# RMS-norm squares kept in fp32 and added in pairs on the vector engine, and buffer slots claimed by the first operation, in an eight-core hybrid decoder step

## The chip, the cores and the metric

The kernel runs on all 8 cores of one Trainium2 chip. Every core runs the same program on its own eighth of the batch: one prompt of 2048 tokens and 16 single-token samples. The metric is device time in microseconds (us) of the slowest core, in one launch. A run can fall into a slow state, in which one die (cores 0 to 3, or 4 to 7) is granted a lower TensorE clock; only fast runs are compared here.

The engines are named as the profile names them: PE is TensorE (matmuls; PEld its weight loads), DVE is VectorE, ACT is ScalarE, POOL is GpSimd, SP issues DMAs.

## The reference, cut to what matters

Four layers, then a final norm. D is 1024, the feed-forward width 2816.

```python
def _rmsnorm(x, g):
    xf = x.astype(jnp.float32)
    y = xf * lax.rsqrt(jnp.mean(xf * xf, axis=-1, keepdims=True) + RMS_EPS)
    return (y * g.astype(jnp.float32)).astype(x.dtype)

# one layer
    h = _rmsnorm(x, norm1_g)                      # "first norm" (n1)
    z = h @ w_in
    zb, zc, zv, zu, ga, gs = jnp.split(z, cuts, axis=-1)
    conv_out, new_buf = _conv_causal(zc * zv, conv_buf, conv_w, conv_b)
    ya = zb * conv_out
    ys, hr, hi = _s5(zu, ...)                     # diagonal state space (SSM)
    gy = jax.nn.gelu(ys, approximate=False)
    ys = gy * jax.nn.sigmoid(gy @ w_glu + b_glu)
    m = jax.nn.sigmoid(ga) * (ya @ w_branch[:512]) + jax.nn.sigmoid(gs) * (ys @ w_branch[512:])
    x = x + m @ w_out
    h2 = _rmsnorm(x, norm2_g)                     # "second norm" (n2)
    gate, up = jnp.split(h2 @ w_gate_up, [D_FF], axis=-1)
    x = x + (jax.nn.silu(gate) * up) @ w_down
```

## The kernel before

Each core keeps x in SBUF in fp32 (tile X), transposed: 128 partitions times 8 chunks of the 1024 model channels, tokens along the free axis. It works through the prompt in two halves of about 1024 tokens. The first half also carries the 16 samples and is cut into three blocks of 384, 384 and 272 columns; the second half into two blocks of 512. A norm therefore has to sum over partitions, which it does with matmuls by a matrix of ones:

```python
    def norm(half, blk, l, which, src=None):
        xin = src or (lambda kt: (X[:, kt, blk.c0:blk.c0 + n], xkeys(kt, blk)))
        ps = PP.new()
        n = blk.n
        hq = lambda kt: (R if which == "fg" else H)[:, kt, blk.c0:blk.c0 + n]     # bf16
        qkeys = rkeys if which == "fg" else hkeys
        for kt in range(8):
            act(lambda e, kt=kt: e.activation(out=hq(kt), in_=xin(kt)[0], func=AF.Square),
                xin(kt)[1], qkeys(kt, blk), n)
            S.pe([(lambda e, kt=kt: e.matmul(ps[:, 0:n], lhsT=ONESB[:], rhs=hq(kt), start=(kt == 0), stop=(kt == 7)),
                   qkeys(kt, blk) + [C_("ONESB")], MMN(n))], [(ps,)], FULL)
        rs = SP_.new()
        # rs = exp(-0.5 * ln(sum / D + eps)): two activations of the "ln" table set
        act(... func=AF.Ln ...); act(... func=AF.Exp, scale=-0.5 ...)
        ...
        for kt in range(8):                       # the "scaling": H = X * g * rs, on DVE
            dve(lambda e, ...: e.scalar_tensor_tensor(out=H[:, kt, ...], in0=xi(), scalar=g, in1=rs[:, 0:n], ...), ...)
```

So a block's norm is 8 squares on ACT (rounded to bf16 into H), 8 ones-matmuls on PE, Ln and Exp on ACT, 8 scalings on DVE, which overwrite H with the normalised input of the next projections.

Nothing is in program order. The operations are recorded with the tiles that they read and write, and a list scheduler orders each engine's queue when the kernel is built. A tile from a pool (`TP` has 4 slots of TB, `SP_` 5 and `SQ` 4 of SC, `PP` the 8 PSUM banks) gets its slot when the first operation that names it is placed; until a slot is free, no operation that names the tile can be placed. The gate projections of the convolution branch are evicted to TB tiles:

```python
            for jj in range(4):
                t_ = tj[jj] = TP.new()
                for blk in blks:
                    pg = projh(uga[jj // 2], jj % 2, blk)      # 8 matmuls into a PSUM bank
                    act(lambda e, ...: e.activation(out=t_[:, ...], in_=pg[:, 0:blk.n], func=AF.Sigmoid), [(pg,)], [(t_, blk.i)], blk.n, tset="sig")
```

The matmuls do not name `t_`, so the scheduler may place them while no TB slot is free, and their PSUM banks then wait full.

Each layer also needs tables for the SSM (complex products of powers of the diagonal). `prep(l)` computes them on DVE and GpSimd with `tt` (fp32 tensor-tensor operations), for layer 0 at the start of the kernel, for the later layers under the feed-forward part of the layer before, in the first half only:

```python
                if half == 0 and l + 1 < DEPTH:
                    span = len(S.ops) - ffn0
                    prep(l + 1, ((ffn0, ffn0 + PS1 * span), (ffn0 + PS1 * span, ffn0 + 0.8 * span)))
```

Of the kernel before, what the change touches and what calls it, by code (L numbers as in the profile page):

```python
# [10 lines left out]
ALU = mybir.AluOpType  # L11
# [65 lines left out]
class Prog:  # L77
    ENGS = ("pe", "act", "dve", "pool", "sp")
    LAT = 0.07
    SWITCH = 1.28  # L80
    MODESW = 0.16
    DBW = 300.0e3
# [94 lines left out]
    def schedule(self):  # L177
# [54 lines left out]
        while nleft:  # L232
# [4 lines left out]
            if isinstance(e, tuple):  # L237
                p, s = e
# [91 lines left out]
                    push(tl.end + self.LAT, (p, tl.slot))  # L330
            for s, i in o.succ:
                s.npred -= 1
                r = o.end + (0.0 if e == "pe" and s.eng == "pe" else self.LAT) - s.offs[i]
                if r > s.ready:
                    s.ready = r
                if s.npred == 0:
                    heapq.heappush(fut[s.eng], (s.ready, s.seq, s))
                    push(max(s.ready, t, efree[s.eng]), s.eng)
# [122 lines left out]
def build():  # L461
# [199 lines left out]

    FULL = (128, 128)

    def proj(parts, blk):
        ps = PP.new()
        nmm = len(parts)
        subs = []
        for i, (u, kw, c, src, keys) in enumerate(parts):
            subs.append((lambda e, u=u, kw=kw, c=c, src=src, i=i: e.matmul(  # L669
                ps[:, 0:blk.n], lhsT=u.ap(kw, c), rhs=src(blk), start=(i == 0), stop=(i == nmm - 1)),  # L670
                [u.key] + keys(blk), MMN(blk.n)))
        S.pe(subs, [(ps,)], FULL)
        return ps

# [9 lines left out]
    def rk(t):  # L684
        return lambda blk: rkeys(t, blk)

    def projh(u, mt, blk):
        return proj([(u, k, mt * 128, hsrc(k), hk(k)) for k in range(8)], blk)

    def projr(u, c, slots, blk):  # L690
        return proj([(u, k, c, rsrc(t), rk(t)) for k, t in enumerate(slots)], blk)
# [1 line left out]
    def norm(half, blk, l, which, src=None):  # L693
        xin = src or (lambda kt: (X[:, kt, blk.c0:blk.c0 + n], xkeys(kt, blk)))
        ps = PP.new()
        n = blk.n
        hq = lambda kt: (R if which == "fg" else H)[:, kt, blk.c0:blk.c0 + n]
        qkeys = rkeys if which == "fg" else hkeys
        for kt in range(8):
            act(lambda e, kt=kt: e.activation(out=hq(kt), in_=xin(kt)[0], func=AF.Square),  # L700
                xin(kt)[1], qkeys(kt, blk), n)
            S.pe([(lambda e, kt=kt: e.matmul(ps[:, 0:n], lhsT=ONESB[:], rhs=hq(kt), start=(kt == 0), stop=(kt == 7)),  # L702
                   qkeys(kt, blk) + [C_("ONESB")], MMN(n))], [(ps,)], FULL)
        rs = SP_.new()
        act(lambda e: e.activation(out=rs[:, 0:n], in_=ps[:, 0:n], func=AF.Ln, bias=CST[:, 0:1], scale=1.0 / D),
            [(ps,), C_("CST")], [(rs,)], n, tset="ln")
        act(lambda e: e.activation(out=rs[:, 0:n], in_=rs[:, 0:n], func=AF.Exp, scale=-0.5), [(rs,)], [(rs,)], n, tset="ln")  # L707
        for kt in range(8):
            xi = lambda kt=kt: xin(kt)[0]
            xik = xin(kt)[1]  # L710
            if which == "fg":
                g = PRM[:, PFG + kt:PFG + kt + 1]
                npr = blk.np
                dve(lambda e, xi=xi, g=g: e.scalar_tensor_tensor(
                    out=xi(), in0=xi(), scalar=g, in1=rs[:, 0:n], op0=ALU.mult, op1=ALU.mult),
                    xik + [(rs,), pk], xik, n, dur=STT_(n), prio=len(S.ops) + (FO if half == 0 else 0))
                S.dma("sp", lambda e, kt=kt: e.dma_start(out=yT[half, :, kt, blk.c0:blk.c0 + npr], in_=X[:, kt, blk.c0:blk.c0 + npr]),
                      [k_ for k_ in xik if k_[2] != 8], [], 128 * npr * 4)
        if which == "fg" and 8 in blk.ss:
            S.dma("sp", lambda e: e.dma_start(out=ysT, in_=X[:, :, 1024:1040]), [("X", k, 8) for k in range(8)], [], 65536)  # L720
        if which != "fg":
            for kt in range(8):
                xi = lambda kt=kt: xin(kt)[0]
                xik = xin(kt)[1]
                g = pcol(l, which, kt)
                dve(lambda e, kt=kt, xi=xi, g=g: e.scalar_tensor_tensor(  # L726
                    out=H[:, kt, blk.c0:blk.c0 + n], in0=xi(), scalar=g, in1=rs[:, 0:n], op0=ALU.mult, op1=ALU.mult),
                    xik + [(rs,), pk], hkeys(kt, blk), n, dur=STT_(n))
# [18 lines left out]
    def prep_body(l):  # L747
# [100 lines left out]
        def prep_f(f):  # L848
# [10 lines left out]
            for h in range(2):  # L859
# [2 lines left out]
                bn16 = lambda bn=bn: bn[:, 0:512].bitcast(BF16).rearrange("p (q r c) -> p q r c", q=4, r=2)  # L862
                bno = lambda ri, bn16=bn16: bn16()[:, :, ri, :].rearrange("p q (c s) -> p q c s", c=16)
                o8 = 8 * h
                tt(zz1, lambda: Bv(me, 0), lambda o8=o8: Pv(pw, o8), ALU.mult, bkk, [(z1,)], 512)
                tt(zz2, lambda: Bv(bct, 256), lambda o8=o8: Pv(me, 512 + o8), ALU.mult, bkk, [(z2,)], 512)
                tt(lambda bno=bno: bno(0), zz1, zz2, ALU.subtract, [(z1,), (z2,)], [(bn, 0)], 512)
                tt(zz2, lambda: Bv(bct, 0), lambda o8=o8: Pv(pw, 256 + o8), ALU.mult, bkk, [(z2,)], 512)
# [109 lines left out]
    def layer(half, l, after_blk, before_fd2=None):  # L978
# [173 lines left out]
        def gas(j4):  # L1152
            uga = [next_unit("ga") for _ in range(2)]
            for jj in range(4):
                t_ = tj[jj] = TP.new()
                for blk in blks:
                    pg = projh(uga[jj // 2], jj % 2, blk)
                    act(lambda e, t_=t_, pg=pg, blk=blk: e.activation(out=t_[:, blk.c0:blk.c0 + blk.n], in_=pg[:, 0:blk.n], func=AF.Sigmoid),  # L1158
                        [(pg,)], [(t_, blk.i)], blk.n, tset="sig")
        for f0 in range(2):  # L1160
# [256 lines left out]
```

## Time and profile before

| | before |
|---|---|
| time, median (range) | 3663.6 us (3660.8 to 3669.5), 3 runs |
| PE busy on the slowest core | 3504.0 us, 96% |
| DVE, ACT, POOL busy | 44%, 31%, 17% |
| ones-matmuls of the norms | 360 |
| waits of PE with a named releaser, mean of the cores | 90.4 us |

These are the lines of the page of the kernel before: the summary of busy times by engine (busy us, share of the span, number of instructions), the clock row of the 40 slices (tenths of full speed), the chain that ended last by line, and the groups of the norm: scaling, squares and ones-matmuls (out<-in, shapes, count | busy us, mean ns of one | idle before and its releaser).

```profile
...
PE 3504.0 (96%) x23912; PEld 1979.7 (54%) x23912; DVE 1618.6 (44%) x2889; ACT 1141.7 (31%) x2151; POOL 608.7 (17%) x799
...
PEclk9799999999999999999999999999999999999999
...
PE ps L669 83%; DMA yT<-X 1%; PE ps L702 1%; PE ps L1107 1%; DVE SC L561 1%; DVE H L726 1%; PE ps L1033 1%; PE ps L908 1%; PE ps L1080 0%; DVE X L1246 0%; DMA scv<-CIN 0%; SPq L632 0%; PE ps L895 0%; DMA X<-xsT 0%; DVE R L1225 0%
...
L700 ACT ACTIVATE H<-X 128x384 bf16<-128x384 f32 (+2 forms) x304 | 156.6, 539 | 198.4 <-DVE X L1246 178.7
L726 DVE SCALAR_TENSOR_TENSOR H<-X,PRM,SC 128x384 bf16<-128x384 f32 (+2 forms) x304 | 183.0, 672 | 35.0 <-ACT SC L707 34.8
...
L702 PE MATMUL ps<-H,ONESB 128*128 128x384 bf16 (+2 forms) x320 | 78.1, 348 | 27.5 <-ACT H L700 26.8
...
```

PE is the bound: 83% of the chain is the projection matmuls of L669. DVE and ACT have more than half of the time free, so work can move from PE to DVE if it does not end up in front of a PE instruction. The ones-matmuls of the squares in H took 78.1 us of PE. The clock row shows one slice below 9: slice 2, about 92 to 183 us, layer 0's table preparation.

These are the waits of PE in layer 0 between its two norms (waiting instruction <- releaser: us in total, times, longest us), and the busy time by engine in 50 to 140 us (start:end length, then busy us and instructions of PE, PEld, DVE, ACT and POOL, the granted clock, DMA share, GB/s).

```profile
...
PE ps L895 <- DVE SC L561: 12.5, 9, 3.0
...
PE ps L895 <- ACT R L775: 6.0, 1, 6.0
PE ps L895 <- ACT TAB L775: 5.8, 1, 5.8
...
```

```profile
...
50.00:140.00 90.00, 51.80 (x592) 34.02 (x592) 83.69 (x128) 37.16 (x74) 34.57 (x30) 0.75 0.50 116
...
```

DVE, which makes the tables, was busy for 83.69 of 90 us, PE for 51.80 of them at a clock of 0.75.

This is the timeline of the last block of a second norm in the first half (start us, length us, engine, line, operation, count, idle before <- releaser).

```profile
...
301.28 0.43 ACT L707 ACTIVATE SC<-SC 128x272 f32<-128x272 f32 x1
...
304.50 1.53 POOL L561 TENSOR_TENSOR TB<-TB 128x512 f32<-128x512 f32 x1 [1.01 <-ACT TAB L889]
...
305.49 1.09 DVE L561 TENSOR_TENSOR TAB<-SC 128x512 bf16<-128x512 f32 x1
306.24 1.47 POOL L561 TENSOR_TENSOR TAB<-TB 128x512 bf16<-128x512 f32 x1 [0.20 <-POOL TB L561]
306.50 5.20 DVE L726 SCALAR_TENSOR_TENSOR H<-X,PRM,SC 128x272 bf16<-128x272 f32 x8
307.84 1.08 POOL L561 TENSOR_TENSOR TB<-TB 128x512 f32<-128x512 f32 x1
...
308.25 0.28 PE L669 MATMUL ps<-H,RING 128*128 128x272 bf16 x1 [2.38 <-DVE H L726]
...
309.37 6.94 PE L669 MATMUL ps<-H,RING 128*128 128x272 bf16 x25 [0.84 <-DVE H L726]
...
```

PE stood still for 2.38 and 0.84 us until the scalings had filled H. Their factor rs was ready long before: its Exp (L707) ended at 301.71. The first scaling began 4.8 us later, because DVE still had preparation (L561) and feed-forward work placed ahead of it in its queue.

### The profile page before, as it was taken

What the parts mean: (1) busy time and instruction counts of PE and PEld (TensorE: products, weight loads), DVE (VectorE), ACT (ScalarE), POOL (GpSimd) and SP (SyncE); (2) the same over time, 40 slices, a digit from 0 to 9 for tenths busy, and PEclk for the clock granted to TensorE, in tenths of its full rate; (3) what the DMA queues carried; (4) which work ended last, traced back from release to release, by engine and by line L of the source; (5) the groups of instructions that cost most, each with busy time, mean ns of one, the idle gap of its engine ahead of it and who ended that gap; (6) DMA issues with size and microseconds to landing.
All of it is one profiled execution on the core that took longest, in us unless ns stands there. A gap on an engine that the chain in (4) does not pass through costs nothing.

```text
span 3663.7 us, 67385 instructions; the slowest of 8 cores (3647.5 to 3663.7 us)
## 1 busy us (share of the span) xinstructions
PE 3504.0 (96%) x23912; PEld 1979.7 (54%) x23912; DVE 1618.6 (44%) x2889; ACT 1141.7 (31%) x2151; POOL 608.7 (17%) x799
## 2 busy tenths in 40 slices
PE   6699999999999999999999899999999999999998
PEld 3466666666666666666664344444444444444443
DVE  8745555465454654543244331354224442254313
ACT  4443234332353322533134320243103421042202
POOL 4232210322103221030000200002000110002000
PEclk9799999999999999999999999999999999999999
DMA  7444557435574355854338544574445644474443
GB/s 157 115 82 70 114 139 149 87 66 113 138 155 86 62 113 135 185 110 84 70 71 196 116 77 71 98 169 74 75 77 115 144 70 81 70 146 79 79 72 87
DMA packets 252804, 384.14 MB, mean 105 GB/s; under 512 B 157632, under 2 KB 180800, under 8 KB 246848
## 3 DMA queue, kind: packets, MB, share of 16 engines
q0 software_dynamic: 67968, 243.30, 39.5%
q1 hardware_dynamic: 184512, 136.53, 12.8%
q8 instruction: 202, 3.31, 0.4%
q14 instruction: 122, 1.00, 0.1%
HBM read 567.06 MB, written 56.12 MB: 170 GB/s over the span
## 4 chain that ended last, share of the span: by engine, by line
PE 88%; DVE 4%; issue 3%; DMA 3%; ACT 1%; SPq 1%; DVEq 0%; ACTq 0%; POOL 0%; POOLq 0%
PE ps L669 83%; DMA yT<-X 1%; PE ps L702 1%; PE ps L1107 1%; DVE SC L561 1%; DVE H L726 1%; PE ps L1033 1%; PE ps L908 1%; PE ps L1080 0%; DVE X L1246 0%; DMA scv<-CIN 0%; SPq L632 0%; PE ps L895 0%; DMA X<-xsT 0%; DVE R L1225 0%
## 5 line engine op out<-in xcount | busy, mean ns | idle before, releaser
L669 PE MATMUL ps<-H,RING 128*128 128x512 bf16 (+2 forms) x12160 | 2194.9, 340 | 23.5 <-DVE H L726 9.7
L669 PEld LDWEIGHTS ps<-H,RING 128*128 128x128 bf16 x12160 | 1191.5, 99 | 965.9 <-issue 52.3
L669 PE MATMUL ps<-R,RING 128*128 128x384 bf16 (+2 forms) x6400 | 1162.1, 339 | 19.7 <-DMA R<-dy 11.4
L669 PEld LDWEIGHTS ps<-R,RING 128*128 128x128 bf16 x6400 | 624.2, 98 | 517.8 <-issue 35.4
L656 POOL DMA_DIRECT2D RING<-wpk x472 | 253.0, 537 | 2635.0 <-PE ps L669 2431.7
L1268 DVE TENSOR_TENSOR R<-SC,ps 128x384 bf16<-128x384 f32 (+2 forms) x440 | 255.8, 583 | 786.7 <-PE ps L669 773.6
L1267 ACT ACTIVATE SC<-ps 128x384 f32<-128x384 f32 (+2 forms) x440 | 226.1, 515 | 1208.0 <-PE ps L669 1199.6
L1246 DVE TENSOR_TENSOR X<-X,ps 128x384 f32<-128x384 f32 (+2 forms) x480 | 269.8, 582 | 448.2 <-PE ps L669 445.2
L700 ACT ACTIVATE H<-X 128x384 bf16<-128x384 f32 (+2 forms) x304 | 156.6, 539 | 198.4 <-DVE X L1246 178.7
L726 DVE SCALAR_TENSOR_TENSOR H<-X,PRM,SC 128x384 bf16<-128x384 f32 (+2 forms) x304 | 183.0, 672 | 35.0 <-ACT SC L707 34.8
L1240 POOL TENSOR_TENSOR R<-TB,SC 128x384 bf16<-128x384 f32 (+1 forms) x160 | 168.1, 1063 | 113.1 <-DVE SC L1237 101.4
L1237 DVE TENSOR_TENSOR SC<-SC,ps 128x384 f32<-128x384 f32 (+1 forms) x160 | 92.7, 584 | 163.5 <-PE ps L669 78.6
L1236 ACT ACTIVATE SC<-ps 128x384 f32<-128x384 f32 (+1 forms) x160 | 81.4, 515 | 248.2 <-PE ps L669 219.8
L1213 DVE TENSOR_TENSOR TB<-TB,ps 128x384 f32<-128x384 f32 (+2 forms) x160 | 89.9, 582 | 128.6 <-PE ps L669 124.6
L1172 DVE TENSOR_TENSOR CIN<-ps,SC 128x384 f32<-128x384 f32 (+2 forms) x80 | 47.0, 587 | 200.7 <-ACT SC L1171 192.6
L561 DVE TENSOR_TENSOR SC<-TB 128x512 f32<-128x512 f32 (+1 forms) x160 | 124.1, 785 | 8.1 <-PE ps L908 0.6
L1158 ACT ACTIVATE TB<-ps 128x384 f32<-128x384 f32 (+1 forms) x160 | 78.9, 516 | 85.8 <-PE ps L669 85.4
L702 PE MATMUL ps<-H,ONESB 128*128 128x384 bf16 (+2 forms) x320 | 78.1, 348 | 27.5 <-ACT H L700 26.8
L561 POOL TENSOR_TENSOR TB<-TB 128x512 f32<-128x512 f32 (+1 forms) x72 | 89.3, 1242 | 42.3 <-DVE R L835 20.7
L1225 DVE TENSOR_TENSOR R<-R,SC 128x384 bf16<-128x384 bf16 (+2 forms) x80 | 46.4, 588 | 88.8 <-ACT SC L1223 86.7
L899 ACT ACTIVATE TAB<-ps 128x512 bf16<-128x512 f32 x60 | 35.5, 597 | 133.0 <-PE ps L895 132.8
L1171 ACT ACTIVATE SC<-ps 128x384 f32<-128x384 f32 (+2 forms) x80 | 41.0, 513 | 95.7 <-PE ps L669 95.5
(180 smaller groups left out, 1633.1 us busy)
## 6 DMA issues: line engine op xcount, KB each, us to landing
RING<-wpk POOLq DMA_DIRECT2D x440, 512.0 KB, 7.0
TAB<-stash SPq DMA_DIRECT2D x21, 1792.0 KB, 10.0
stash<-TAB SPq DMA_DIRECT2D x15, 1792.0 KB, 7.6
R<-stash SPq DMA_DIRECT2D x7, 1792.0 KB, 14.8
RING<-wpk POOLq DMA_DIRECT2D x32, 384.0 KB, 6.1
du<-R SPq DMA_DIRECT2D x32, 256.0 KB, 9.2
UU<-du SPq DMA_DIRECT2D x32, 256.0 KB, 7.2
dy<-YY SPq DMA_DIRECT2D x32, 256.0 KB, 6.6
```

The costliest lines, as they stand in the source:

```text
L561: fn = lambda e: e.tensor_tensor(out=out(), in0=a(), in1=b(), op=op)
L656: S.dma("pool", lambda e: e.dma_start(out=t[:, 0:n], in_=wpk[l, ui, :, 0:n]), [("X",) + gate] if gate else (), [(t,)], 128 * n * 4, prio=- ...
L669: subs.append((lambda e, u=u, kw=kw, c=c, src=src, i=i: e.matmul(ps[:, 0:blk.n], lhsT=u.ap(kw, c), rhs=src(blk), start=(i == 0), stop=(i = ...
L700: act(lambda e, kt=kt: e.activation(out=hq(kt), in_=xin(kt)[0], func=AF.Square), xin(kt)[1], qkeys(kt, blk), n)
L702: S.pe([(lambda e, kt=kt: e.matmul(ps[:, 0:n], lhsT=ONESB[:], rhs=hq(kt), start=(kt == 0), stop=(kt == 7)), qkeys(kt, blk) + [C_("ONESB")] ...
L726: dve(lambda e, kt=kt, xi=xi, g=g: e.scalar_tensor_tensor(out=H[:, kt, blk.c0:blk.c0 + n], in0=xi(), scalar=g, in1=rs[:, 0:n], op0=ALU.mul ...
L1213: dve(lambda e, po=po, n=n, t_=t_, blk=blk: e.tensor_tensor(out=t_[:, blk.c0:blk.c0 + n], in0=t_[:, blk.c0:blk.c0 + n], in1=po[:, 0:n], op ...
L1237: dve(lambda e, sg=sg, po=po, n=n: e.tensor_tensor(out=sg[:, 0:n], in0=sg[:, 0:n], in1=po[:, 0:n], op=ALU.mult), [(sg,), (po,)], [(sg,)], n)
L1240: S.op(MENG, lambda e, sg=sg, n=n, t_=t_, blk=blk, j=j: e.tensor_tensor(out=R[:, MT[j], blk.c0:blk.c0 + n], in0=t_[:, blk.c0:blk.c0 + n], ...
L1246: dve(lambda e: e.tensor_tensor(out=X[:, j, blk.c0:blk.c0 + n], in0=X[:, j, blk.c0:blk.c0 + n], in1=ps[:, 0:n], op=ALU.add), [(ps,)] + xke ...
L1267: act(lambda e, sg=sg, pg=pg, n=n: e.activation(out=sg[:, 0:n], in_=pg[:, 0:n], func=AF.Silu), [(pg,)], [(sg,)], n, tset="silu")
L1268: dve(lambda e, sg=sg, pu=pu, n=n, blk=blk, ti=ti: e.tensor_tensor(out=R[:, ti, blk.c0:blk.c0 + n], in0=sg[:, 0:n], in1=pu[:, 0:n], op=ALU ...
```

## The change

The intent is to halve the ones-matmuls: the squares of two chunks are kept in fp32 (in SC tiles), added on DVE, rounded once into bf16, and one ones-matmul takes the sum. Left as they were are the first norm of layer 0 (the start), the norm at the change of halves that reads a staged input, and the final norms. Besides, an operation that fills a PSUM bank for a TB slot now names the TB tile ("own"), so that it is placed only when the slot is there. `LATPE` has the value of `LAT` and changes nothing.

```diff
-    def proj(parts, blk):
+    def proj(parts, blk, own=()):
 ...
-                [u.key] + keys(blk), MMN(blk.n)))
+                [u.key] + keys(blk) + list(own), MMN(blk.n)))
 ...
+        pairs = which != "fg" and src is None and not (half == 0 and l == 0 and which == "n1")
+        QP = SQ if half == 1 else SP_
+        for k2 in range(4 if pairs else 0):
+            ta, tb2 = QP.new(), QP.new()
+            for t, kt in ((ta, 2 * k2), (tb2, 2 * k2 + 1)):
+                act(lambda e, kt=kt, t=t: e.activation(out=t[:, 0:n], in_=xin(kt)[0], func=AF.Square), xin(kt)[1], [(t,)], n)
+            tt(lambda k2=k2: hq(k2), lambda ta=ta: ta[:, 0:n], lambda tb2=tb2: tb2[:, 0:n], ALU.add, [(ta,), (tb2,)], qkeys(k2, blk), n)
+            S.pe([(lambda e, k2=k2: e.matmul(ps[:, 0:n], lhsT=ONESB[:], rhs=hq(k2), start=(k2 == 0), stop=(k2 == 3)),
+                   qkeys(k2, blk) + [C_("ONESB")], MMN(n))], [(ps,)], FULL)
-        for kt in range(8):
+        for kt in range(0 if pairs else 8):
 ...                                              # table preparation
-                tt(zz1, ..., ALU.mult, bkk, [(z1,)], 512)
+                tt(zz1, ..., ALU.mult, bkk + [(tab, "own")], [(z1,)], 512)
 ...                                              # gate projections
-                    pg = projh(uga[jj // 2], jj % 2, blk)
+                    pg = projh(uga[jj // 2], jj % 2, blk, [(t_, "own")])
```

More of the change, by code (lines that the diff above doesn't have):

```diff
@@ L79 @@
     LAT = 0.07
+    LATPE = 0.07
     SWITCH = 1.28
@@ L332, in schedule @@
                 s.npred -= 1
-                r = o.end + (0.0 if e == "pe" and s.eng == "pe" else self.LAT) - s.offs[i]
+                r = o.end + (0.0 if e == "pe" and s.eng == "pe" else self.LATPE if s.eng == "pe" else self.LAT) - s.offs[i]
                 if r > s.ready:
@@ L685, in rk, with projh @@
         return lambda blk: rkeys(t, blk)
-    def projh(u, mt, blk):
-        return proj([(u, k, mt * 128, hsrc(k), hk(k)) for k in range(8)], blk)
+    def projh(u, mt, blk, own=()):
+        return proj([(u, k, mt * 128, hsrc(k), hk(k)) for k in range(8)], blk, own)
     def projr(u, c, slots, blk):
@@ L864, in prep_f @@
                 o8 = 8 * h
-                tt(zz1, lambda: Bv(me, 0), lambda o8=o8: Pv(pw, o8), ALU.mult, bkk, [(z1,)], 512)
+                tt(zz1, lambda: Bv(me, 0), lambda o8=o8: Pv(pw, o8), ALU.mult, bkk + [(tab, "own")], [(z1,)], 512)
                 tt(zz2, lambda: Bv(bct, 256), lambda o8=o8: Pv(me, 512 + o8), ALU.mult, bkk, [(z2,)], 512)
```

## The prediction

-25 for PE, -5 for layer 0 and 0 to +4 for the tails make -30 to -26, from 3664 us; the text says "about -30" and 3634.

> **What bounds it now.** TensorE. On the slowest core the page gives PE 3504 of 3664 us (96%), DVE 44%, ACT 31%; the chain of waits is 88% PE, 83% of the span the projection matmuls. In long runs a 512-column matmul starts every 216 ns (1008 in 217.59 us, chain in order of time). [...] The rest, about 160 us of idle PE plus time at a low clock, sits in few places (waits of PE; busy time by stretches): the first norm; table preparation in layer 0, 50 to 140 us, PE busy 52 of 90 us at a granted clock of 0.75 while DVE is busy 84; some 3.3 us before the last block of the second norm in three first-half layers; some 20 us at the half change.
>
> **What changes.** 35 norm blocks (21 in the first half, 14 in the second) send 4 sums to the ones-matmul instead of 8: 140 matmuls fewer, 140 vector adds more, the same squares on ACT.
> - PE: 84 matmuls in the first half (two thirds 384 columns, one third 272), 56 of 512 columns. At the groups' busy time per matmul (172, 135, 220 ns) 13.4 + 12.3 = 26 us.
> - DVE: an fp32 add should cost as the existing fp32 tensor-tensor ops: 690, 552, 436 ns at 512, 384, 272. Sum 82 us. Off the chain except at a norm's last pair, about +0.6 us.
> - ACT: the built order has 7 more switches from silu to ln and back; in the second half Ln and Exp of the second norm's last block are now split by silus. About 6 us more before that block's H is ready; but PE's order puts 9 first-block projection groups (15.5 us) after the last norm matmul where it had 4, so I expect little stall.
> - Slots first: gate projections of layer 0 no longer sit in PSUM waiting for a TB slot. PE's order has 10 to 12 more conv groups (1.1 us each) inside the DVE-bound preparation. With 13 us more DVE work there, I count 5 us. At the half change the order is the same: its idle time stays.
>
> **On the critical path.** Nearly all the PE saving, as the norm matmuls stand in dense streams: −25. Layer 0: −5, could be −15 or +5. Norm tails and DVE pressure where preparation shares DVE: 0 to +4. Sum about −30: **3634 us, 0.8% less; range 3610 to 3656**. Faster by over 2%: 0.04; within 2%: 0.95; slower: 0.01.
>
> **What would show it.** Norm matmuls 360 to 220, their busy time from about 87 us to about 55. PE busy falls by 20 to 30 us with the span; DVE up by 80. Adds of 0.44 to 0.69 us. In layer 0 PE does more within 50 to 140 us at a better clock. Second-half steady layers (428 to 431 us apart) about 3 us shorter. PE's waits for H in the second norm stay near 3 us in the first half, small in the second.
>
> **What would make it wrong.** The adds queue on DVE (in order) behind preparation or eviction work and the ones-matmul stalls PE's stream. Or the split Ln/Exp starves PE in the second-half layers (4 x 3 us). Or layer 0's new order lengthens preparation.

## The result, and the profile after

The changed kernel takes 3628.72 us (median of 4 runs, 3627.59 to 3631.75), the kernel before 3662.24 (median of 4, 3660.78 to 3669.47). The ratio of the fast runs is 0.9906, with a 95% interval of 0.9889 to 0.9923: 0.9% less time, within 2%. A ratio here is always the mean time of one kernel's fast runs over that of the other's of the same rounds, so it is not quite the ratio of the medians quoted.

The same lines of the page after. L705 are the paired squares, L562 with H<-SC the adds, L707 the ones-matmuls of the pairs and L712 those that stayed; the lines by form follow in the second fence.

```profile
...
PE 3473.9 (96%) x23772; PEld 1960.4 (54%) x23772; DVE 1691.4 (47%) x3029; ACT 1147.2 (32%) x2158; POOL 609.1 (17%) x799
...
PEclk9899999999999999999999999999999999999999
...
PE ps L670 83%; DMA dy<-YY 1%; PE ps L1117 1%; DVE H L736 1%; ACT SC L1233 1%; PE ps L707 1%; DVE SC L562 1%; PE ps L1043 1%; PE ps L1090 1%; PE ps L918 0%; DMA scv<-CIN 0%; DVE R L1235 0%; SPq L633 0%; PE ps L905 0%; DMA R<-dy 0%
...
L705 ACT ACTIVATE SC<-X 128x384 f32<-128x384 f32 (+2 forms) x280 | 147.2, 543 | 205.0 <-DVE X L1256 178.7
L736 DVE SCALAR_TENSOR_TENSOR H<-X,PRM,SC 128x384 bf16<-128x384 f32 (+2 forms) x304 | 190.9, 698 | 27.4 <-ACT SC L717 27.4
...
L562 DVE TENSOR_TENSOR H<-SC 128x384 bf16<-128x384 f32 (+2 forms) x140 | 81.3, 590 | 36.2 <-ACT SC L705 36.2
...
```

```profile
...
L707 PE MATMUL ps<-H,ONESB 128*128 128x512 bf16 x56 | 18.1, 378 | 0.6
...
L707 PE MATMUL ps<-H,ONESB 128*128 128x384 bf16 x56 | 16.0, 326 | 2.5 <-DVE H L562 2.5
...
L712 PE MATMUL ps<-H,ONESB 128*128 128x384 bf16 x16 | 7.1, 480 | 19.6 <-ACT H L710 19.6
L707 PE MATMUL ps<-H,ONESB 128*128 128x272 bf16 x28 | 6.7, 278 | 0.2
...
```

PE has 140 matmuls fewer and 30 us less busy time; the pair matmuls take 18.1 + 16.0 + 6.7 = 40.8 us. The 140 adds take 81.3 us on DVE. The clock of slice 2 went from 0.7 to 0.8. Layer 0 and the busy times in its stretch:

```profile
...
PE ps L905 <- DVE SC L562: 14.9, 7, 4.3
...
PE ps L918 <- ACT SC L1199: 1.3, 1, 1.3
...
```

```profile
...
50.00:140.00 90.00, 64.60 (x781) 42.89 (x782) 87.36 (x140) 41.09 (x84) 33.03 (x28) 0.83 0.58 121
...
```

The waits for R and TAB of L775, 6.0 and 5.8 us before, are no longer among the long ones, and PE does 781 matmuls instead of 592 in the same 90 us, at a clock of 0.83.

The tail of the second norm, the same place as before:

```profile
...
292.52 1.76 DVE L562 TENSOR_TENSOR SC<-TB 128x512 f32<-128x512 f32 x1
...
293.87 5.20 POOL L562 TENSOR_TENSOR TB<-TB 128x512 f32<-128x512 f32 x4
...
294.20 7.88 DVE L736 SCALAR_TENSOR_TENSOR H<-X,PRM,SC 128x272 bf16<-128x272 f32 x8
...
295.75 0.28 PE L670 MATMUL ps<-H,RING 128*128 128x272 bf16 x1 [0.45 <-DVE H L736]
...
297.07 0.28 PE L670 MATMUL ps<-H,RING 128*128 128x272 bf16 x1 [1.04 <-DVE H L736]
...
298.29 0.28 PE L670 MATMUL ps<-H,RING 128*128 128x272 bf16 x1 [0.95 <-DVE H L736]
...
299.27 1.26 POOL L562 TENSOR_TENSOR TAB<-TB 128x512 bf16<-128x512 f32 x1 [0.20 <-POOL TB L562]
...
```

The eight scalings now take 7.88 instead of 5.20 us, with five GpSimd products beside them instead of two (four that write TB and one that writes TAB), and PE takes one matmul at a time, as H comes. One by one in this trace, each of the five scalings that ran beside a product took 1.30 to 1.54 us and ended 0.30 us after that product; each of the last three, with no product beside it, took 0.49. The scalings again begin late, but less so: Exp ended at 291.46 (its line is shown with the sixth experiment), so it is 2.7 us now.

Where did the time go? The start of the first block's Ln is a mark that every norm of both kernels has. The table gives the stretches between these marks in the profiled runs, as means of all 8 cores, and in the last column the change of "matmul time": for every matmul of the stretch the time to the next at full clock, (columns + 6)/2.4 ns and at least 26.7 ns. That is an estimate, a straight line through the median intervals in the two traces: 216 ns from a matmul of 512 columns to the next, 162 for 384, 116 for 272, 56 for 128; the floor lies between the 25 ns (16 columns) and 28 ns (64 columns) of the small ones that the page gives as 128*128. For the other tiny ones of the SSM it is rough (those of 64 columns often follow each other in 9 to 28 ns). Two of the 8 traces lack 166 matmul records in every kernel, so sums are some 9 us low and differences stand.

| stretch | before | after | change | of it matmul time |
|---|---|---|---|---|
| start to layer 0's second norm | 274.7 | 264.5 | -10.2 | +0.8 |
| first half, second norm to next first norm, 3 | 781.5 | 777.3 | -4.2 | -5.3 |
| first half, first norm to second norm, 3 | 599.5 | 599.5 | 0.0 | -5.6 |
| layer 3's second norm, over the half change, to layer 0's second norm | 459.9 | 454.7 | -5.2 | -1.4 |
| second half, second norm to next first norm, 3 | 706.5 | 702.6 | -3.9 | -1.9 |
| second half, first norm to second norm, 3 | 575.6 | 563.9 | -11.7 | -8.4 |
| last feed-forward, final norm, end | 258.2 | 255.3 | -2.9 | -2.6 |
| sum | 3655.9 | 3618.0 | -38.0 | -24.4 |

Two things stand out besides the matmuls: layer 0, and a scatter in the stretches with the SSM (first to second norm). The latter comes from waits of PE that have no releaser in the profile ("issue"), here one in each kernel:

```profile
...
597.17 0.20 PE L1033 MATMUL ps<-UU,TAB 128*64 128x64 bf16 x1
602.06 0.60 PE L1043 MATMUL ps<-UU,TAB 128*64 128x16 bf16 x15 [4.69 <-issue]
...
```

```profile
...
590.34 0.18 PE L1103 MATMUL ps<-UU,TAB 128*128 128x16 bf16 x1 [3.48 <-issue]
...
600.28 0.47 PE L1117 MATMUL ps<-VT,TAB 64*128 64x64 bf16 x20 [3.53 <-issue]
...
```

In the kernel before this wait follows the same matmul, number 4328 in PE's order, on all 8 cores (4.6 us on average); in the changed kernel two waits follow numbers 4352 and 4475, again on all 8 cores. In PE's instruction stream (two instructions for a matmul: weights and product) all the long waits that the 8 cores share stand at the same place of a block of 256 (instruction 187 to 189), and the two waits of the changed kernel are 123 matmuls, one block, apart. The queue that moves instructions agrees in count (queue, kind: packets, MB, share of 16 engines):

```profile
...
q8 instruction: 202, 3.31, 0.4%
...
```

```profile
...
q8 instruction: 200, 3.28, 0.4%
...
```

The built PE programs have 51,810 and 51,259 instructions: divided by 256, 202.4 and 200.2. So a packet goes with a block of 256 instructions; 3.31 MB in 202 packets are 16.4 KB each. One packet of this queue moved within each of the waits shown: from 599.7 to 600.6 us in the one that ended at 602.06, and in the changed kernel from 587.5 to 589.0 and from 597.6 to 598.7 us in those that ended at 590.34 and 600.28. In these two traces (the six cores of each with all matmul records) PE had no such wait (0.25 us or more, no releaser) at the end of a block that had lasted 13 us or more (none of 1933); a block that PE used up in under 4 us, as happens in the SSM stretches, was always followed by one (22 of 22, 1.3 to 4.3 us). The removal of 140 matmuls moves every later block end relative to the work, so each stretch wins or loses a few us by where the ends fall.

This is PE's time by kind, in us, as mean of the 8 cores of the profiled run. A wait counts from 0.25 us, and "issue" has waits without a releaser, or with PE itself. "Slow" is the time lost, within 8 us after a wait of that kind, to matmuls that start over half as late again as at full clock; part of it is the halved clock after a stall (matmuls of 512 columns that start every 427 ns instead of 216, at a granted clock of 0.50, in 2412.6 to 2415.5 us of the kernel before), part is pacing by operands in pieces under 0.25 us. The first wait of PE, for the first data, is not counted. Smaller gaps and slow time elsewhere (55.9 and 53.7 us) are left out.

| kernel | matmul time | waits with releaser | slow after them | issue waits | slow after them |
|---|---|---|---|---|---|
| before | 3463.7 | 90.4 | 36.2 | 16.9 | 12.8 |
| after | 3439.2 | 79.0 | 32.9 | 20.8 | 14.3 |

So 24.5 us (24.4 by the table of stretches) came from matmuls, 11.4 from waits, 3.3 from the slow time after them, and 5.4 were lost again at and after issue waits: 33.8 of the 38.0 us.

### The profile page after: what moved, and what is told of

Same layout as the page of the kernel before. It is cut to its first block, busy times and chain, and to the rows that moved or that the text cites. A ratio compares the mean times of both kernels' runs of the same rounds, so it can differ in the third digit from the quotient of the medians.

```text
span 3626.0 us, 67081 instructions; the slowest of 8 cores (3611.5 to 3626.0 us)
## 1 busy us (share of the span) xinstructions
PE 3473.9 (96%) x23772; PEld 1960.4 (54%) x23772; DVE 1691.4 (47%) x3029; ACT 1147.2 (32%) x2158; POOL 609.1 (17%) x799
## 3 DMA queue, kind: packets, MB, share of 16 engines
q0 software_dynamic: 67968, 243.30, 40.8%
q1 hardware_dynamic: 184512, 136.53, 12.9%
## 4 chain that ended last, share of the span: by engine, by line
PE 87%; DVE 4%; issue 4%; DMA 2%; ACT 2%; SPq 1%; DVEq 0%; POOL 0%; ACTq 0%; POOLq 0%
PE ps L670 83%; DMA dy<-YY 1%; PE ps L1117 1%; DVE H L736 1%; ACT SC L1233 1%; PE ps L707 1%; DVE SC L562 1%; PE ps L1043 1%; PE ps L1090 1%; PE ps L918 0%; DMA scv<-CIN 0%; DVE R L1235 0%; SPq L633 0%; PE ps L905 0%; DMA R<-dy 0%
## 5 line engine op out<-in xcount | busy, mean ns | idle before, releaser
L670 PE MATMUL ps<-H,RING 128*128 128x384 bf16 (+2 forms) x12160 | 2196.5, 340 | 30.1 <-DVE H L736 14.2
L705 ACT ACTIVATE SC<-X 128x384 f32<-128x384 f32 (+2 forms) x280 | 147.2, 543 | 205.0 <-DVE X L1256 178.7
L736 DVE SCALAR_TENSOR_TENSOR H<-X,PRM,SC 128x384 bf16<-128x384 f32 (+2 forms) x304 | 190.9, 698 | 27.4 <-ACT SC L717 27.4
L562 DVE TENSOR_TENSOR SC<-TB 128x512 f32<-128x512 f32 (+1 forms) x160 | 121.1, 767 | 5.6
L562 POOL TENSOR_TENSOR TB<-TB 128x512 f32<-128x512 f32 (+1 forms) x72 | 89.9, 1253 | 69.7 <-DVE TB L562 52.1
L562 DVE TENSOR_TENSOR H<-SC 128x384 bf16<-128x384 f32 (+2 forms) x140 | 81.3, 590 | 36.2 <-ACT SC L705 36.2
```

The source lines that it names most:

```text
L562: fn = lambda e: e.tensor_tensor(out=out(), in0=a(), in1=b(), op=op)
L670: subs.append((lambda e, u=u, kw=kw, c=c, src=src, i=i: e.matmul(ps[:, 0:blk.n], lhsT=u.ap(kw, c), rhs=src(blk), start=(i == 0), stop=(i = ...
L705: act(lambda e, kt=kt, t=t: e.activation(out=t[:, 0:n], in_=xin(kt)[0], func=AF.Square), xin(kt)[1], [(t,)], n)
L736: dve(lambda e, kt=kt, xi=xi, g=g: e.scalar_tensor_tensor(out=H[:, kt, blk.c0:blk.c0 + n], in0=xi(), scalar=g, in1=rs[:, 0:n], op0=ALU.mul ...
```

## The experiments

All kernels gave correct results. In each of the three calls (the first four experiments, the next four, the last three) many runs were slow, 3 to 5 of 11 of the kernel before; they are left out; "core mean" is the mean span of the cores on undisturbed dies, over all runs of the kernel in its call, with its standard error of about 1 us. The kernel before has a core mean of 3654.8 in the first call, 3659.0 in the second and 3655.0 in the third.

The theory after the result: (a) a ones-matmul taken out of a dense stream is worth its whole time, in both halves; (b) layer 0 gains from the gate projections' claim, not from the pairs; (c) the tails of the second norm in the first half are set by DVE's scalings, which are slow while GpSimd's products run; (d) the rest is block ends of the instruction stream. Rivals: the pairs gain by relieving ACT or the norm's chain instead of PE; layer 0 gains from its norms; the tails wait for Ln and Exp, which the new order splits, or for other work that stands ahead of the scalings in DVE's queue; the issue waits belong to the work at their places.

### Pairs without the claims

```diff
-    bkk + [(tab, "own")]
+    bkk
-    pg = projh(uga[jj // 2], jj % 2, blk, [(t_, "own")])
+    pg = projh(uga[jj // 2], jj % 2, blk)
```

> Pairs without the early slot claims: layer 0 keeps the order of before. Theory (two additive parts, about 24 us of tensor-engine time from 140 matmuls fewer, and about 10 us from the claim of TB slots in layer 0): 3662 becomes 3636 to 3642, ratio 0.993 to 0.995, and layer 0 up to the first Ln of its second norm stays near 253 us as in before. Rival (the gain is mostly the new order in layer 0, and the matmul saving is given back as waits for the adds): 3652 or more, ratio 0.997 or more.

Measured: ratio 0.9966 (0.995 to 0.9982), 3651.0 us as mean of 3 fast runs, core mean 3638.1. Layer 0's second norm came 0.8 us later than before instead of 10.2 earlier, so (b) holds for the pairs' side. The total missed the expectation by some 10 us. Its row in the table of kinds is 3439.2, 90.8, 30.1, 26.4, 17.6: the matmul time is that of the changed kernel to the last digit, the waits with a releaser are those of before, but the issue waits are 9.5 us up on before and the slow time after them 4.8. The pairs alone have bad block ends.

### Claims without the pairs

```diff
-        pairs = which != "fg" and src is None and not (half == 0 and l == 0 and which == "n1")
+        pairs = False
```

By a comparison of the built orders, the claim of the preparation's table changes nothing on any engine; only that of the gate projections acts. No run has one claim without the other.

> Early claims without pairs (eight squares, eight matmuls as before). Built order: only the claim by the gate projections changes any order; the claim of the preparation table changes none. Theory: layer 0 up to the first Ln of its second norm is about 10 us shorter than in before (243 against 253), all later stages as in before; 3650 to 3655, ratio 0.996 to 0.998. Rival (claims only make the schedule feasible and are free): 3660 to 3664.

Measured: ratio 0.9993 (0.9974 to 1.0012), 3660.7 us, core mean 3650.6. The total is the rival's, the place is the theory's. Layer 0's second norm came 10.9 us earlier, as the theory said: in its window of 50 to 140 us PE did 788 matmuls, where the pairs alone did 596.

```profile
...
50.00:140.00 90.00, 63.25 (x788) 42.48 (x788) 87.34 (x141) 40.76 (x83) 32.69 (x27) 0.85 0.52 119
...
```

```profile
...
50.00:140.00 90.00, 49.78 (x596) 32.92 (x597) 83.49 (x130) 37.47 (x75) 35.30 (x30) 0.79 0.53 113
...
```

But the gain was given back: the stretches from first to second norm of layers 2 and 3 lost 4.2 and 2.5 us, and the half change 4.0. Issue waits were 21.9 us against 16.9, waits with a releaser 82.8. In layers 2 and 3 the loss goes with issue waits (2.1 and 2.2 us more) and the slow time after them. At the half change it does not: there PE waited longer for a DMA (R<-dy, 14.7 us instead of 12.8) and for a TB eviction (4.5 instead of 2.5), and no run shows why. So the gain in layer 0 is real and the total does not show it. The total is a poor judge of a part of this kernel, because each edit also moves the block ends; the stretch is a better one.

### Pair matmuls issued twice

This keeps the adds and the claims, and gives PE its 140 matmuls back. The scheduler still builds a new order around them. The sums double, so Ln's scale is halved.

```diff
-            S.pe([(... matmul(ps, ONESB, hq(k2), start=(k2 == 0), stop=(k2 == 3)) ...)], ...)
+            S.pe([(... matmul(ps, ONESB, hq(k2), start=(k2 == 0), stop=False) ...),
+                  (... matmul(ps, ONESB, hq(k2), start=False, stop=(k2 == 3)) ...)], ...)
-        ... func=AF.Ln, bias=CST[:, 0:1], scale=1.0 / D
+        ... func=AF.Ln, bias=CST[:, 0:1], scale=(0.5 if pairs else 1.0) / D
```

> The change as it is, but each ones-matmul of a pair sum is issued twice (140 matmuls back; Ln's scale is halved, so the result is right). Vector adds and claims stay. Theory (tensor time is what the pairs save): the 24 us come back: 3650 to 3656, within 3 us of the run with claims alone. Rival (the gain of the pairs comes from the squares' new home, fewer waits or the scheduler's luck): stays within 10 us of 3629.

Measured: ratio 0.9971 (0.9947 to 0.9994), 3652.6 us, core mean 3643.4. Against the changed kernel's ratio of 0.9906 that is 0.65%, or 24 us, for 140 matmuls whose time at full clock is 24.5 us. That fits theory (a), but it is weaker than it looks. One of the three fast runs (3662.64) had a die at a clock of 0.98 that was 18 us longer than the other; without it the two ratios differ by 0.5%, or 19 us. And the order was not kept: ACT has 126 table loads instead of 132, and in the first-half tails PE waits 2.0 us for H instead of 4.5. By stretch, the second half after its first mark lost 4.0 us against the changed kernel for 11.2 us of matmul time, the half change 8.0 for 3.3; only the sum, 23.6 for 24.4, agrees. Theory (a) is seen more cleanly where PE has no wait of 0.25 us or more: the last stretch of the table (-2.9 us for -2.6 of matmul time), and the fours below. The expected nearness to the claims alone did not come (7 us less); this kernel's issue waits and waits with a releaser, 21.0 and 75.1 us, were lower by 9 in sum.

### Pairs in the second half only

```diff
-        pairs = which != "fg" and src is None and not (half == 0 and l == 0 and which == "n1")
+        pairs = which != "fg" and src is None and not (half == 0 and l == 0 and which == "n1") and half == 1
```

> Claims, and pairs only in the second half (56 matmuls of 512 columns fewer). Theory: second half gains 12 us and the first-half layers lose what the adds cost there. If pairs are worth 12 us in the first half too, 3640 to 3643; if the first half gives most of it back (waits for H grew from 3.3 to 4.5 us in three layers, layer time hardly fell), the run is only 4 to 8 us slower than the whole change: 3633 to 3637.

Measured: ratio 0.9946 (0.9931 to 0.9961), 3643.7 us, core mean 3631.5. The total is just above the first of the two cases expected. The first half's pairs are worth 0.40%, some 14 us, near their 12 us of matmul time; they are not eaten by the shared preparation.

### 128 no-ops ahead of PE's program

```diff
+            for _ in range(128 if e == "pe" else 0):
+                eng.nop()
             for o in self.order[e]:
```

> The change, with 128 no-ops at the start of the tensor engine's program and nothing else. In before and in the change its waits with the releaser 'issue' begin at instruction 187 or 188 of a block of 256 of its program, on all cores at the same matmul (4352, 4475, 7798, 7921, 11738 in the change). Theory (PE waits there for the next 16 KB block of its program): the waits stand at instruction 187 or 188 again, so at other matmuls, about 62 earlier or later; their sum (21 us in the change) moves by up to 8 us, and time with it: 3617 to 3636; every other stage keeps its length. Rival (a wait for data or a semaphore that the trace does not show): the waits stay at the matmuls named, and the time is 3627 to 3631.

Measured: ratio 0.9898 (0.988 to 0.9916), core mean 3616.5. No operation moved in the order. The waits at matmuls 4352, 4475, 7798, 7921 and 11738 were gone and stood at 4413, 4537, 7983, 8106 and 11552, each half a block or one and a half (a half is 61 to 62 matmuls) from an old place; two of these were seen on all 8 cores, three on 5 or 6. Here are the first two, 4413 on the slowest core and 4537 on core 1:

```profile
...
599.58 0.22 PE L1045 MATMUL ps<-UU,R 128*64 128x64 bf16 x2 [2.02 <-issue]
...
```

```profile
...
600.03 3.89 PE L672 MATMUL ps<-H,RING 128*128 128x384 bf16 x14 [0.79 <-issue]
...
```

Issue waits fell from 20.8 to 16.1 us in sum, and single stretches moved by -4.4, +6.2 and -5.5 us. Theory (d) holds: the waits belong to block ends, not to the work. The total moved by less than the noise, since wins and losses cancelled.

### Ln and Exp of the second norm next to each other on ACT

The built order of the changed kernel splits Ln and Exp of a second norm's last block by silu work, which costs table loads. Two of them stand here between Ln (L715) and Exp (L717), where the expectation below says four:

```profile
...
287.43 0.49 ACT L715 ACTIVATE SC<-ps,CST 128x272 f32<-128x272 f32 x1
287.94 1.28 ACT L1277 ACT_TABLE_LOAD   x1
...
289.23 0.49 ACT L1277 ACTIVATE SC<-ps 128x384 f32<-128x384 f32 x1
289.74 1.28 ACT L717 ACT_TABLE_LOAD   x1
291.03 0.43 ACT L717 ACTIVATE SC<-SC 128x272 f32<-128x272 f32 x1
...
```

The edit makes the scheduler place the Exp right after its Ln and gives both a higher priority, for the second norm only.

```diff
+            if e == "act" and must is not None:   # take only the Exp that belongs to the last Ln
+                ...
-            [(ps,), C_("CST")], [(rs,)], n, tset="ln")
+            [(ps,), C_("CST")], [(rs,)], n, tset="ln", prio=len(S.ops) + S.shift - 200 if which == "n2" else None)
```

> The change, with Ln and Exp of the second norm back to back on ACT and ahead of silus (139 switches of table set instead of 153). Theory (PE waits for the last block's H in three first-half layers, 4.5 us each, because silus and four table loads stand between Ln and Exp and bring the scaling on DVE late, into the GpSimd products): PE's waits for H there fall from 13.5 us in sum to 6 or less, the three stages from second norm to next first norm (259 us) shorten by 3 to 4 us each; 3615 to 3622. Rival (the scaling operations themselves, about 1 us each behind GpSimd, set the wait): waits stay above 11 us, 3626 to 3632.

Measured: ratio 0.9903 (0.9886 to 0.992), core mean 3620.5; no gain. The page counts 118 table loads instead of 132, the three stretches from second to next first norm were 2.1 to 2.6 us shorter, PE's wait for H there fell from 4.5 to 3.1 us each, but the scalings kept their pace of 0.98 us, and other stretches gave it back (issue waits 23.5 us). The scalings now begin 0.25 us after the end of Exp instead of 2.7, so this edit also took the work ahead of them out of DVE's queue. So the split and the queue together explain 1.4 of 4.5 us of the wait, not the bulk; both expectations for the wait (6 us or less, over 11 us in sum) were missed, as it was 9.2.

### GpSimd's products held until the norm's last scaling

```diff
+                    p0 = len(S.ops)
                     prep(l + 1, ((ffn0, ffn0 + PS1 * span), (ffn0 + PS1 * span, ffn0 + 0.8 * span)))
+                    for o in S.ops[p0:]:
+                        if o.eng == "pool" and not o.dma:
+                            o.deps.append((S.ops[ffn0 - 1], 0))      # the norm's last scaling
```

The theory tested is that the scalings are slow because GpSimd's products run beside them.

> The change, with the GpSimd products of the next layer's preparation held until the last scaling of the second norm is done. Theory [...]: the eight 272-column scalings of the last block take 0.58 to 0.65 us each instead of 0.98, PE's waits for H there fall from 13.5 us in sum to below 8; 3619 to 3626. Rival (scalings are slow for another reason): they stay near 0.98 us and the time stays at 3627 to 3632.

Measured: ratio 0.9861 (0.9845 to 0.9877), 3617.4 us as mean of 4 fast runs, core mean 3605.3: better than expected. The scalings:

```profile
...
293.33 3.39 DVE L736 SCALAR_TENSOR_TENSOR H<-X,PRM,SC 128x272 bf16<-128x272 f32 x8 [1.12 <-ACT SC L717]
...
296.93 1.59 POOL L562 TENSOR_TENSOR TB<-TB 128x256 f32<-128x256 f32 x2 [15.09 <-DVE H L736]
...
```

Eight scalings take 3.39 us, 0.42 each, where they took 7.88; GpSimd begins after them, and PE no longer waits for H. The three stretches are 7.3, 6.4 and 7.0 us shorter than in the changed kernel; of this 4.5 us is the wait, the rest the slow time after it. The five scalings beside a product in the changed kernel each took 1.30 to 1.54 us and ended 0.30 us after it; here, without products, the pace is 0.42 us. X and rs, their inputs, both lie in SBUF, and the traces of the two kernels under study (all 8 cores) show the same of DVE's other work there: a tensor-tensor operation of 512 fp32 columns with both inputs in SBUF took 0.69 us (median of 4738) with no tensor-tensor operation of GpSimd beside it and 1.37 us (median of 539) with one beside it for over 80% of its time; with one input in PSUM it took 0.69 us either way (10,000 and 456). What mechanism is behind it the traces do not show. The edit did a second thing, though: DVE's share of the preparation waits for the products, so it left the queue ahead of the scalings too, which begin 0.10 us after the end of Exp instead of 2.7. Together with the run before, where that delay was gone and the wait still 3.1 us, the larger part of the wait in the changed kernel belongs to the pace.

### Both of these

```diff
                     prep(l + 1, ...)
+                    # every GpSimd operation of prep: o.deps.append((S.ops[ffn0 - 1], 0))
-            [(ps,), C_("CST")], [(rs,)], n, tset="ln")          # Ln, and its Exp placed right after it
+            [(ps,), C_("CST")], [(rs,)], n, tset="ln", prio=len(S.ops) + S.shift - 200 if which == "n2" else None)
```

> Ln and Exp together and the GpSimd products held, both. If the two causes act on the same wait, no more than the better of the two: waits for H below 4 us in sum, 3613 to 3621. Preparation starts later, which may lengthen its end: if the stages from first norm to second norm (201 us) grow by more than 2 us, the holding costs something there.

Measured: ratio 0.9858 (0.9843 to 0.9874), core mean 3605.2, the same as with the products alone. PE has no wait for H left with either, so the two edits remove the same wait. By stretch, both together are still 1.1 to 1.2 us shorter at each of the three places, and issue waits (27.4 against 23.4 us) take it back. Of the stages from first to second norm, one grew by 2.8 us over the changed kernel, past the 2 us of the expectation, the others by 1.6 and 0.3; with the products alone it was 2.7, 0.6 and -0.4. Whether that is the later preparation or block ends was not tested.

### The kernel before with GpSimd's products held

```diff
                     prep(l + 1, ...)
+                    # every GpSimd operation of prep: o.deps.append((S.ops[ffn0 - 1], 0))
```

The theory is the same, (c).

> The kernel before, with only the GpSimd products of the next layer's preparation held until the last scaling of the second norm. Theory [...]: the eight 272-column scalings take 0.42 us each instead of 0.65, the three PE waits for H of 3.2 us go, and the three stages from a second norm to the next first norm shorten by 4 to 5 us each, less than the 6.4 to 7.4 us that the same edit gave in the changed kernel, because there the pair adds had pushed the scalings deeper into the products. Core mean 3643 to 3650, ratio 0.996 to 0.999. Rival (the products' delay helps in some other way, such as the order in the next layer): the same 14 us as in the changed kernel, ratio 0.9955 or lower, or no shortening of just those stages.

Measured: ratio 0.9939 (0.9924 to 0.9953), 3642.2 us, core mean 3633.2. The number is the rival's, the place is the theory's: just the three stretches from second to next first norm shortened, by 7.4, 7.6 and 7.9 us, every other stretch is within 1.2 us of before, and the issue waits stayed (16.8 against 16.9 us). This is the cleanest pair, as PE's instruction count is unchanged. It does not separate two causes, however: the scalings take 3.39 us instead of 5.20, and they begin 0.10 us after the end of Exp instead of 4.8, since the preparation's DVE work has left the queue ahead of them. In the kernel before, that late start alone is longer than PE's wait of 3.2 us.

```profile
...
299.77 16.45 PE L669 MATMUL ps<-H,RING 128*128 128x384 bf16 x114
...
301.55 3.39 DVE L726 SCALAR_TENSOR_TENSOR H<-X,PRM,SC 128x272 bf16<-128x272 f32 x8 [0.47 <-ACT SC L707]
...
305.15 1.58 POOL L561 TENSOR_TENSOR TB<-TB 128x256 f32<-128x256 f32 x2 [12.39 <-ACT SC L1267]
...
```

PE runs 114 matmuls without a break where it had stood still. Its row is 3463.7, 81.7, 26.0, 16.8, 12.1: the waits fell by 8.7 us and the slow time after them by 10.2. The expectation had counted the waits alone. It was also wrong that the pairs had made the tail dearer: the same edit gains as much with the pairs as without. PE waits 1.3 us longer for H with them, but in more and shorter pieces, and the slow time after them is shorter.

### Squares added in fours, with the products held

Six adds and two ones-matmuls a block instead of four and four.

```diff
-        for k2 in range(4 if pairs else 0):
-            ...                                      # 2 squares, 1 add, 1 matmul
+        for k4 in range(2 if pairs else 0):
+            acc = QP.new()
+            sq(4 * k4, acc)                          # the square on ACT, in fp32
+            for j in range(1, 4):
+                tb2 = QP.new()
+                sq(4 * k4 + j, tb2)
+                tt(hq(k4) if j == 3 else acc, acc, tb2, ALU.add)       # shortened
+            S.pe([(... matmul(ps, ONESB, hq(k4), start=(k4 == 0), stop=(k4 == 1)) ...)], ...)
```

> The gated changed kernel, with the squares of a block added in fours: 6 adds and 2 ones-matmuls for each block instead of 4 and 4. PE has 70 matmuls fewer, about 12 us at their busy times; DVE has 70 adds more, about 41 us at 590 ns each. Theory (a matmul less in a dense stream is worth its whole time, a DVE add off the chain nothing): core mean 3593 to 3599, ratio 0.982 to 0.985. Rival (DVE has been brought to where its order binds: chains of three adds make the ones-matmul wait): core mean 3603 or more, ratio 0.9855 or more, with waits of PE for the H of the adds. Places of instruction-block waits move again and may hide up to 6 us either way.

Measured: ratio 0.981 (0.9796 to 0.9825), 3594.5 us as mean of 4 fast runs, median 3595.94: better than expected, and the fastest kernel. Relative to the kernel before in its own rounds the core mean is 68.4 us less, against 53.7 for the pairs with the products held. Of the 14.7 us between them 12.2 are matmul time (3427.0 against 3439.2); the issue waits were also lower, 17.6 against 23.4. The DVE has 48% busy and its longer chains show up as this wait of PE:

```profile
...
PE ps L711 <- DVE H L562: 6.5, 9, 1.0
...
```

It is 6.5 us, with no piece over 1.0; in the pairs with the products held it was 2.5 us. A matmul moved to DVE still pays at this point. Where PE has no waits, the stretches shrink by nearly the matmul time: against the pairs with the products held, the second half's stretches from second to next first norm are 7.8 us shorter for 8.5 of matmul time, the last stretch 2.5 for 2.8. That is the clearest evidence for theory (a).

### Products held, with the 128 no-ops

```diff
                     prep(l + 1, ...)
+                    # every GpSimd operation of prep: o.deps.append((S.ops[ffn0 - 1], 0))
+            for _ in range(128 if e == "pe" else 0):
+                eng.nop()
             for o in self.order[e]:
```

> The gated changed kernel with 128 no-ops at the start of PE's program, so that its 256-instruction blocks end 128 instructions earlier in the work. Theory of instruction-block waits: the waits without a releaser, 23.4 us in sum for the gated kernel, move by about 60 matmuls in the small-matmul stages, and their sum falls as it did for the changed kernel (20.8 to 16.1), so core mean 3599 to 3605 and ratio 0.984 to 0.986. Rival (those waits belong to the work at those places, not to block ends): they stay at the same matmules and the ratio is that of the gated kernel within 0.0005.

Measured: ratio 0.9828 (0.9813 to 0.9844), 3601.2 us, core mean 3591.3: 10 us less than without the no-ops, relative to before in their own rounds, and better than both expectations. The issue waits moved to the places of the other shifted kernel (4413, 4537, 7983, 8106, 11552) and fell from 23.4 to 14.9 us, the slow time after them from 15.7 to 11.3. Where the ends of 256-instruction blocks fall is worth some 10 us here, more than a quarter of the change under study. It is luck, and no edit of this kernel aims at it.

## Why the prediction was right

The time was predicted as 3634 us, with 3610 to 3656 as range; it is 3628.7. Point by point:

- *PE, -25 us: right.* 140 matmuls fewer, 24.5 us of matmul time; putting them back cost 19 to 24 us in total, in an order that was not quite the same. The busy time of the norm's matmuls fell less than was said: by their groups from 88.7 to 65.4 us instead of 87 to 55. Those two figures lay 32 us apart, more than the 26 us that the prediction itself had added up; the measured 23.3 is near the sum, not near the pair. PE's busy time fell by 30 us (20 to 30 predicted).
- *DVE, 82 us of adds: right.* 81.3 us, 689, 567 and 437 ns at 512, 384 and 272 columns; in the kernel before the tensor-tensor operations of L1268 on fp32 inputs took 688, 552 and 436 ns. DVE as a whole rose by 73 us. That the adds are nearly off the chain is shown by the fours, where PE waits 6.5 us for them in all.
- *ACT, 7 more table loads: right,* 125 before and 132 after on the page, and nothing lost: the kernel with 118 of them was as fast. The 6 us that the prediction saw ahead of a last block's H in the second half were its estimate; from the end of Ln to the Exp it was 0.6 us before and 3.2 after. In the second half PE has no wait of 0.25 us or more for the H of a second norm, as predicted.
- *Layer 0, -5 us: right in cause, too small.* It gave -10.2, as a whole from the gate projections' claim (-10.9 with the claims alone, +0.8 with the pairs alone). The prediction priced the conv groups that move forward and took half back for 13 us more DVE work in the stretch. It was not taken back: as means of the cores, the waits for R and TAB of L775 fell from 6.0 and 5.5 us to nothing and 1.5, which is the gain, while DVE was busy for 87.4 of 90 us instead of 83.7 without a longer stretch.
- *Norm tails, 0 to +4 us: right in size, wrong in mechanism.* The three stretches lost 1.1 us against their matmul time. PE's wait for H did not stay "near 3 us": it rose from 3.2 to 4.5. The prediction named DVE's queue. That queue was there in both kernels, but it got shorter: between the end of Exp and the first scaling lay 4.8 us before and 2.7 after. What grew is the scalings' own time, 5.20 to 7.88 us, because in the new order five of them instead of two fell beside GpSimd products, which the prediction did not have. How the wait of the kernel before divides between queue and products was not tested: holding the products removes both.
- *Half change: right in the main.* The DMA wait there stayed, 12.8 before and 12.9 us after on average. Not all of its idle time stayed, though: the stretch gained 3.8 us beyond its matmuls, most of it in a wait for a TB eviction (2.5 to 0.8) and in slow time (3.9 to 2.5).
- *Second-half layers about 3 us shorter: right on average only.* From second norm to second norm they are 3.7, 10.7 and 1.0 us shorter, with 3.5 us of matmul time each. The scatter is block ends of the instruction stream, which the prediction did not have at all.

So the total was met by terms of the right kind, with layer 0 some 5 us better than priced. What the prediction lacked, block ends, cost 5.4 us in the changed kernel and could have cost 14, as in the pairs alone. That the result lies only 5 us from the predicted number is luck: layer 0 and the block ends were each missed by some 5 us, with opposite sign.

What stays open: how much of the gain from holding the products is the faster pace of the scalings and how much is the emptier queue of DVE; which of the moved groups of layer 0 filled which wait (no run moved them one by one), and when the next block of instructions is called for. Blocks that lasted between 4 and 13 us were waited for in some cases and not in others, and no run measured that by itself.

## What to carry to other kernels

On an engine that is busy 96% of the time in dense streams, work taken off it was worth nearly its whole time here, and the idle engine that took it over cost little as long as it did not stand before one of its instructions: 140 matmuls gave some 24 us, 70 more gave 12 to 15. A stall of the matmul engine at the end of a norm cost about twice its length here (holding the products took 8.7 us of waits and 10.2 us of slow time after them from the kernel before), so look at what feeds it there, keep vector operations with both inputs in SBUF apart from GpSimd products (1.37 us beside one, 0.69 without, for 512 columns), and look at what stands ahead of them in the vector engine's queue (both together 6 to 8 us for each place). Where stretches of tiny matmuls exist, judge an edit by the stretch it acts on and not by the total, which block ends of the instruction stream can move by 10 us.

## Other measurements of this case

- Block ends of the instruction stream: in stretches of small matmuls PE waits 1.7 to 4.6 us (mean of the cores) at such a place, in the two kernels under study on all 8 cores at the same matmul; such waits sum to 15 to 27 us in a run, and the slow time after them adds 11 to 18. 128 no-ops moved the places by 61 to 62 matmuls.
- The clock after a stall: a count over the traces of the two kernels under study, all 8 cores of each, takes stalls of PE that have no other of 0.25 us or more within 8 us and mostly large matmuls after them. It calls a stall followed by the half pace when matmuls of 272 to 512 columns, starting at about double interval, lost over 0.8 us in the next 6 us. That holds for none of 102 stalls of 0.5 to 1 us, none of 7 of 1.5 to 2 us, 9 of 16 of 2 to 2.5 us, 11 of 11 of 2.5 to 3 us and 30 of 32 of 3 to 4 us; the 6 of over 4 us lost 2.3 us (median). Many are the same place on several cores and in both kernels. At the half pace a 512-column matmul started every 0.427 us after a stall of 1.78 us in the kernel before (which had another, of 2.15 us, 3.7 us earlier), and every 0.216 us in long runs.
- DVE and GpSimd side by side: eight 272-column scalings took 3.39 us alone, 5.20 or 7.88 us beside GpSimd products of 1.1 to 1.5 us.
- Table loads of ACT: each takes 1283 ns, and the switch in the lines above cost no more than that: an activation that ended at 287.92 us was followed by a load from 287.94 to 289.22 and the next activation at 289.23.
- Build-time order and block ends act together: parts of a change that gave ratios of 0.9966 and 0.9993 alone gave 0.9906 together.
